# Sample-row fp32 products placed in the four column quarters of the TensorE array

## The chip, the cores and the metric

The kernel runs on one core of a Trainium2 chip. The metric is the device time of one execution in microseconds (us), from the median of several runs. A profile of one execution comes from the hardware profiler; in it PE is the matmul side of TensorE, PEld its weight loads, DVE is VectorE, ACT is ScalarE, POOL is GpSimd, and SP issues most DMAs.

## What is computed

One layer of a hybrid decoder works on 1024 prompt tokens and on 8 sample rows (eight sequences with one new token each), with shared weights. After an RMS norm and a wide input projection come two branches: retention (4 heads, keys of 128, values of 256, with a state matrix per head) and sliding-window attention (16 query heads in 4 groups that share a key/value head, head size 64, window 128). Each branch is normalised or gated and projected; the two are merged and projected again.

The change concerns only the 8 sample rows. Each of them has its own state and its own cache, so that its products share nothing with the other rows:

```python
def retention_chunk(S, q, k, v, lg):            # sample rows: L = 1, S is (8, heads, 128, 256)
    ...
    S_new = exp(L*lg) * S + einsum('bmhd,bmhe,mh->bhde', k, v, k_dec)
    o = ... einsum('bnhd,bhde->bnhe', q, S) ... # per sample: a 1 x 128 row times its 128 x 256 state

def swa_sample(q, k, v, sinks, cache_k, cache_v):
    kk = concatenate([cache_k, k]); vv = concatenate([cache_v, v])
    s = einsum('bnqhgd,bnkhd->bnhgqk', q, kk) * 64**-0.5   # per sample and kv head: 4 x 64 times 64 x 128
    p = softmax(with the sink)                              # 32 rows of 128 per kv head
    return einsum('bnhgqk,bnkhd->bnqhgd', p, vv)            # per sample: 4 x 128 times 128 x 64
```

## The kernel before

Nearly all of the time is the big projections, each product of which is done in three fp32r matmuls (high times high, high times low, low times high). `phase1` makes the normed input, then runs eight groups, four retention heads and four key/value heads of the window branch; `phase23` runs the branch projections and the output projection. Within a group, `groups` appends steps: a gemm for one 128-token tile, the generator steps of the tiles before it (`ret_tile`, `swa_tile`), gate blocks as filler, and the sample rows of the group at one place in it (`ret_rows`, `swa_rows`), which are generators too, advanced one `yield` at a time. The final order of the instructions on each engine is not the order of the code: a scheduler places them by a simulated timeline, and each engine works its own list in order.

The sample rows of a retention head (`ret_rows`, L394 to L447): the row projection, eight outer products into the state (L426, L428), and then in two halves of four samples the products of query and state. All four write to the same 8 rows of PSUM: sample b's weights are an 8-column block, `zq`, that holds its query in column b and zeros elsewhere (made by one multiplication with a mask, L432), and the four are added up in PSUM:

```python
for b in range(H):                                                      # L440
    nc.tensor.matmul(po[:NS, :DV], zq[:, half * H + b, :], st[:, b, :], start=(b == 0), stop=(b == H - 1))
```

The two halves are added on 8 rows (L444, L446), and `head_norm` normalises and transposes them (L339).

The sample rows of a key/value head (`swa_rows`, L573 to L630): queries are transposed (L591) and masked into `zq` (L594), the cached keys of two samples at a time are transposed into a 128 x 128 block (L600). The scores of all 32 rows (8 samples, 4 heads) come from four matmuls that are added up on the same 32 rows of PSUM (L607). After the softmax on 32 rows a transpose (L615), and one matmul of 32 rows against the values of all eight samples, 512 columns (L620), of which a mask (L622) and a sum (L624) keep each row's own 64. The result is transposed (L627) and copied to `oT` (L630).

All operands of L441, L607 and L620 are plain fp32, and each such matmul stands in the trace as two loads and two matmul records: the two passes of one product. Of the big gemms (fp32r) each has one. "128*8" in a row of the profile means 128 rows and 8 columns of the array in use.

Of the kernel before, what the change touches and what calls it, by code (L numbers as in the profile page):

```python
# [12 lines left out]
AF = mybir.ActivationFunctionType  # L13
ALU = mybir.AluOpType
AX = mybir.AxisListType
# [31 lines left out]
MROW = 40  # L47
MLO = 32
KST = 64 + NS

RAW = 3
NA1 = 7
# [20 lines left out]
def shape_constants():  # L73
    c, s = rope_tables(DK)
    out = {}
    cols = SEQ + NS
    ct = np.concatenate([c[:cols].T, c[:cols].T], 0)
    st = np.concatenate([s[:cols].T, -s[:cols].T], 0)
    out["c_ropeT"] = np.stack([ct, st], 1)
    tm = np.concatenate([c, s], 1).reshape(NT + 1, P, 128)  # L80
    tm[NT] *= DK ** -0.5
    out["c_ropeK"] = tm.transpose(1, 0, 2)
    c2, s2 = rope_tables(HD)
    tm = np.concatenate([c2, s2], 1).reshape(NT + 1, P, HD)
# [9 lines left out]
    misc = np.zeros((P, 8 + 8 + 64 + 128 + 8))  # L94
# [5 lines left out]
    misc[:, 16:80] = np.eye(8).reshape(1, 64)  # L100
    z = np.zeros((2, HD, NS // 2, NS, G))
    for b in range(NS):
        z[b % 2, :, b // 2, b, :] = 1.0
    misc[:, 80:208] = z.reshape(P, 128)
    for r in range(NS * G):
        misc[r, 208 + r // G] = 1.0
    out["c_misc"] = misc
    return {k: np.ascontiguousarray(v.astype(np.float32)) for k, v in out.items()}

# [13 lines left out]
class Body:  # L123
# [200 lines left out]
    def head_norm(self, po, p, c, oT, cols):  # L324
        nc = self.nc
        junk = self.t(self.ap, [P, DV], "junk", bufs=1)
        ss = self.t(self.sm, [P, 1], "ss", bufs=4)
        nc.scalar.activation(out=junk[:p], in_=po, func=AF.Square, scale=c, accum_out=ss[:p])
        r = self.rstd(ss[:p], DV, 1, 1.0, p)
        if not isinstance(c, float):  # L330
            f = self.t(self.sm, [P, 1], "fsc", bufs=4)
            nc.vector.tensor_tensor(out=f[:p], in0=r, in1=c, op=ALU.mult)
            r = f[:p]
        on = self.t(self.ap, [P, DV], "on", bufs=1)
        nc.scalar.activation(out=on[:p], in_=po, func=AF.Copy, scale=r)
# [4 lines left out]
        nc.vector.tensor_copy(out=oT[:, :, cols], in_=pt[:, : 2 * P].rearrange("p (i n) -> p i n", i=2)[:, :, :p])  # L340

    def ret_tile(self, h, t, units, qT, st, oT):
        nc = self.nc
# [50 lines left out]
    def ret_rows(self, h, units, qT, oT):  # L394
# [23 lines left out]
        for half in range(2):  # L418
# [9 lines left out]
                nc.vector.scalar_tensor_tensor(out=sl, in0=sl, scalar=self.g1[h], in1=ps[:], op0=ALU.mult, op1=ALU.add)  # L428
            yield
            if half == 0:  # L430
                zq = self.t(self.ap, [P, NS, NS], "zq", bufs=1)
                nc.vector.tensor_tensor(  # L432
                    out=zq[:],
                    in0=qT[:, SEQ:TOK].unsqueeze(1).broadcast_to([P, NS, NS]),
                    in1=self.misc[:, 16:80].rearrange("p (a b) -> p a b", a=NS),
                    op=ALU.mult,
                )
                osum = kv[:, :DV]
            po = self.t(self.pav, [P, 512], "av")
            for b in range(H):  # L440
                nc.tensor.matmul(po[:NS, :DV], zq[:, half * H + b, :], st[:, b, :], start=(b == 0), stop=(b == H - 1))  # L441
            nc.sync.dma_start(out=self.o["rs"][0, bs, h].rearrange("b d e -> d b e"), in_=st[:])
            if half == 0:
                nc.scalar.activation(out=osum, in_=po[:NS, :DV], func=AF.Copy)  # L444
            else:
                nc.vector.tensor_tensor(out=osum, in0=osum, in1=po[:NS, :DV], op=ALU.add)  # L446
        yield from self.head_norm(osum, NS, 1.0, oT, slice(SEQ, TOK))  # L447


    def rope_s(self, dst, src, A, B, nh, t, p=P):  # L450
# [122 lines left out]
    def swa_rows(self, g, units, oT):  # L573
# [18 lines left out]
        zq = self.t(self.ap, [P, NS // 2, NS, G], "zq2", bufs=1)  # L592
        qv = pt[:, : G * NS].rearrange("p (j b) -> p b j", j=G).unsqueeze(1).broadcast_to([P, NS // 2, NS, G])
# [10 lines left out]
        R = NS * G  # L604
# [3 lines left out]
        s = self.t(self.ap, [R, 1, P], "srow", bufs=1)  # L608
        mx = self.t(self.sm, [P, 4], "mx", bufs=2)
        nc.vector.tensor_copy(out=s[:, 0, :], in_=sc[:R, :P])  # L610
        nc.vector.tensor_reduce(out=mx[:R, 0:1], in_=s[:, 0, :], axis=AX.X, op=ALU.max)
        self.softmax_tail(s, [s[:, 0, :]], [1.0], mx[:R, 0:1], self.nsinkr[:, g : g + 1], self.sinkr[:, g : g + 1], R, 1)
# [3 lines left out]
        pTs = self.t(self.ap, [P, R], "pTs", bufs=1)  # L616
        nc.scalar.activation(out=pTs[:], in_=pt[:, :R], func=AF.Copy)
# [5 lines left out]
        os_ = self.t(self.ap, [R, HD], "osr", bufs=1)  # L623
# [4 lines left out]
        pv = pt[:HD, :R].rearrange("p (b i a) -> p i b a", b=NS, i=2)  # L628
        for a in range(2):
            nc.vector.tensor_copy(out=oT[a * HD : (a + 1) * HD, :, SEQ:TOK], in_=pv[:, :, :, a])  # L630

    def swa_tables(self):
        nc = self.nc
# [22 lines left out]
    def build(self):  # L656
# [4 lines left out]
        with tc.tile_pool(name="const", bufs=1, reuse_waits="tile") as cp, tc.tile_pool(name="sm", bufs=2, reuse_waits="tile") as sm, \  # L661
# [9 lines left out]
            self.misc = self.t(cp, [P, 216], "misc")  # L671
# [23 lines left out]
    def groups(self):  # L695
# [157 lines left out]
    def swa_consts(self):  # L853
# [11 lines left out]
        nc.sync.dma_start(out=self.sink[:], in_=self.i["swa_sinks"][0:1, :].broadcast_to([P, SH]))  # L865
        self.nsink = self.t(ap, [P, SH], "nsink")
        nc.vector.tensor_scalar(out=self.nsink[:], in0=self.sink[:], scalar1=-1.0, scalar2=None, op0=ALU.mult)
        self.sinkr = self.t(ap, [NS * G, KVH], "sinkr")
        for b in range(NS):
            nc.sync.dma_start(out=self.sinkr[b * G : (b + 1) * G, :], in_=self.i["swa_sinks"][0].rearrange("(g j) -> j g", g=KVH))  # L870
        self.nsinkr = self.t(ap, [NS * G, KVH], "nsinkr")
# [126 lines left out]
```

## Time and profile before

| | |
|---|---|
| median of 3 runs | 1188.66 us (1185.74 to 1190.13) |
| profiled execution | 1189.96 us, its span 1188.1 us |
| busy: PE / PEld | 1166.6 us / 1103.2 us |
| busy: DVE / ACT / POOL | 644.3 / 438.7 / 429.0 us |
| DMA | mean 98 GB/s, 116.61 MB |
| granted TensorE clock | 0.997 of full speed |

A timeline row reads: start, how long from the first start to the last end, engine, line, operation, output <- inputs, array rows*columns, partitions x elements, count; in brackets, idle time before it and what ended it. A matmul record lasts from its start to its modelled end and overlaps the next one, so what a matmul costs the engine is the distance from its start to the next start.

### The profile page before, as it was taken

What the parts mean: (1) busy time and instruction counts of PE and PEld (TensorE: products, weight loads), DVE (VectorE), ACT (ScalarE), POOL (GpSimd) and SP (SyncE); (2) the same over time, 40 slices, a digit from 0 to 9 for tenths busy, and PEclk for the clock granted to TensorE, in tenths of its full rate; (3) what the DMA queues carried; (4) which work ended last, traced back from release to release, by engine and by line L of the source; (5) the groups of instructions that cost most, each with busy time, mean ns of one, the idle gap of its engine ahead of it and who ended that gap; (6) DMA issues with size and microseconds to landing.
All of it is one profiled execution on the core that took longest, in us unless ns stands there. A gap on an engine that the chain in (4) does not pass through costs nothing.

```text
span 1188.1 us, 19187 instructions
## 1 busy us (share of the span) xinstructions
PE 1166.6 (98%) x7116; PEld 1103.2 (93%) x7116; DVE 644.3 (54%) x1798; ACT 438.7 (37%) x1130; POOL 429.0 (36%) x395
## 2 busy tenths in 40 slices
PE   6999999999999999999999999999999999999998
PEld 5899999999989999999999999999999999999876
DVE  5755545544644386776775677477843411654121
ACT  6533333344234235544463446345544210221010
POOL 5325116215325435533563356235751221221010
PEclk9999999999999999999999999999999999999999
DMA  9224114313123411220141014101537744644221
GB/s 321 59 73 115 60 43 146 113 60 94 49 69 84 136 63 46 74 79 7 59 129 43 10 60 126 47 1 37 174 104 242 232 143 138 187 127 142 74 91 69
DMA packets 125165, 116.61 MB, mean 98 GB/s; under 512 B 17480, under 2 KB 113224, under 8 KB 125040
## 3 DMA queue, kind: packets, MB, share of 16 engines
q1 hardware_dynamic: 118160, 106.93, 29.2%
q10 hardware_dynamic: 6912, 8.46, 2.0%
q8 instruction: 56, 0.92, 0.3%
q14 instruction: 37, 0.30, 0.1%
HBM read 84.98 MB, written 32.44 MB: 99 GB/s over the span
## 4 chain that ended last, share of the span: by engine, by line
PE 92%; DMA 2%; DVE 2%; issue 1%; ACT 1%; POOL 1%; SPq 0%; ACTq 0%; POOLq 0%
PE acc L212 16%; PE acc L213 16%; PE acc L214 16%; PE acc L224 10%; PE acc L223 10%; PE acc L222 10%; PE acc L233 1%; PE acc L232 1%; PE sc L532 1%; PE av L441 1%; PE sc L533 1%; PE av L564 1%; PE av L565 1%; PE tr L544 1%; DMA oT<-d_o 1%
## 5 line engine op out<-in xcount | busy, mean ns | idle before, releaser
L169 POOL TENSOR_TENSOR wlo<-wraw,whi 128x1024 fp32r<-128x1024 f32 (+1 forms) x92 | 206.7, 2253 | 311.7 <-ACT whi L168 268.8
L212 PE MATMUL acc<-hhi,whi 128*128 128x344 f32 x864 | 279.9, 324 | 2.0 <-ACT tg L298 2.0
L214 PE MATMUL acc<-hhi,wlo 128*128 128x344 f32 x864 | 277.5, 322 | 0.0
L213 PE MATMUL acc<-hlo,whi 128*128 128x344 f32 x864 | 277.1, 321 | 0.0
L222 PE MATMUL acc<-whi,hhi 128*128 128x384 f32 x512 | 175.6, 344 | 2.3 <-ACT hhi L139 1.2
L224 PE MATMUL acc<-whi,hlo 128*128 128x384 f32 x512 | 175.3, 342 | 0.0
L223 PE MATMUL acc<-wlo,hhi 128*128 128x384 f32 x512 | 175.3, 343 | 0.0
L212 PEld LDWEIGHTS acc<-hhi,whi 128*128 128x128 f32 x864 | 162.9, 188 | 5.5 <-ACT tg L298 2.6
L213 PEld LDWEIGHTS acc<-hlo,whi 128*128 128x128 f32 x864 | 162.6, 188 | 1.6
L214 PEld LDWEIGHTS acc<-hhi,wlo 128*128 128x128 f32 x864 | 162.6, 188 | 1.6 <-issue 0.4
L168 ACT ACTIVATE whi<-wraw 128x1024 fp32r<-128x1024 f32 (+1 forms) x92 | 90.4, 984 | 177.3 <-PE acc L213 114.3
L147 POOL TENSOR_TENSOR rs<-ms,nhalf 128x1 f32<-128x1 f32 (+3 forms) x81 | 69.4, 858 | 216.7 <-DVE ms L146 192.4
L222 PEld LDWEIGHTS acc<-whi,hhi 128*128 128x128 f32 x512 | 97.5, 191 | 6.1 <-issue 2.5
L224 PEld LDWEIGHTS acc<-whi,hlo 128*128 128x128 f32 x512 | 97.3, 190 | 0.5 <-DVE hlo L140 0.2
L223 PEld LDWEIGHTS acc<-wlo,hhi 128*128 128x128 f32 x512 | 97.4, 190 | 0.4
L288 POOL TENSOR_TENSOR oT<-oT,tg 128x344 f32<-128x344 f32 x48 | 48.3, 1007 | 63.1 <-DVE tg L286 58.6
L486 ACT ACTIVATE s<-sc,ng,rs 128x128 f32<-128x128 f32 x128 | 57.0, 456 | 17.4 <-DVE ng L483 17.3
L224 PE MATMUL acc<-whi,mlo 128*128 128x512 f32 x128 | 50.5, 395 | 0.0
L223 PE MATMUL acc<-wlo,mhi 128*128 128x512 f32 x128 | 50.3, 393 | 0.0
L222 PE MATMUL acc<-whi,mhi 128*128 128x512 f32 x128 | 50.1, 393 | 0.0
L965 DVE TENSOR_TENSOR x<-acc,x 128x512 f32<-128x512 f32 x16 | 11.0, 690 | 68.7 <-PE acc L224 68.7
L286 DVE SCALAR_TENSOR_TENSOR tg<-tg,acc 128x344 f32<-128x344 f32 x48 | 24.5, 511 | 35.7 <-ACT tg L285 35.5
(357 smaller groups left out, 2394.8 us busy)
## 6 DMA issues: line engine op xcount, KB each, us to landing
wraw<-in_w_in SPq DMA_DIRECT2D x36, 512.0 KB
d_t<-tg ACTq DMA_DIRECT2D x48, 172.0 KB
d_o<-oT SPq DMA_DIRECT2D x16, 516.0 KB
tt<-d_t SPq DMA_DIRECT2D x48, 172.0 KB
wraw<-in_w_in SPq DMA_DIRECT2D x32, 256.0 KB
st<-d_o SPq DMA_DIRECT2D x9, 516.0 KB
d_m<-tt SPq DMA_DIRECT2D x24, 172.0 KB
mm<-d_m SPq DMA_DIRECT2D x24, 172.0 KB
```

The costliest lines, as they stand in the source:

```text
L147: nc.gpsimd.tensor_tensor(out=rs[:p, :width], in0=ms[:p, :width], in1=self.nhalf[:p, :width], op=ALU.pow)
L168: nc.scalar.activation(out=hi[:, :f], in_=raw[:, :f], func=AF.Copy)
L169: nc.gpsimd.tensor_tensor(out=lo[:, :f], in0=raw[:, :f], in1=hi[:, :f].bitcast(F32), op=ALU.subtract)
L212: nc.tensor.matmul(ps, whi[:, k, :], hi[:, cs], start=(k == 0), stop=False)
L213: nc.tensor.matmul(ps, whi[:, k, :], lo[:, cs], start=False, stop=False)
L214: nc.tensor.matmul(ps, wlo[:, k, :], hi[:, cs], start=False, stop=(k == KT - 1))
L222: nc.tensor.matmul(ps, hi[:, k, a:b], whi[:, kk, :], start=(k == 0), stop=False)
L223: nc.tensor.matmul(ps, hi[:, k, a:b], wlo[:, kk, :], start=False, stop=False)
L224: nc.tensor.matmul(ps, lo[:, k, a:b], whi[:, kk, :], start=False, stop=(k == KT - 1))
L286: nc.vector.scalar_tensor_tensor(out=tg[:], in0=tg[:], scalar=1.0, in1=ps[:, :BL], op0=ALU.add, op1=ALU.mult)
L288: nc.gpsimd.tensor_tensor(out=sl, in0=sl, in1=tg[:], op=ALU.mult)
L486: nc.scalar.activation(out=s[:p, j, :], in_=src[j], func=AF.Exp, bias=ng[:p, j : j + 1], scale=scale[j], accum_out=l[:p, j : j + 1])
```

## The change

Four products at a time are written to different quarters of the array's columns, 32 columns each (`tile_position=(0, 32 * b)`), and so to different quarters of the 128 PSUM partitions, rather than being added up on the same rows.

- `ret_rows`: `zq` becomes a lasting tile with 32 columns per sample, zeroed once; each head copies its queries into one column of each. Each half's four products go to quarters 0 to 3; half 0 stands in row 0 of a quarter, half 1 in row 1. The copy, the sum and `head_norm` work on 128 partitions, and the transposes of `head_norm` are 128 wide, with two copies that pick the rows.
- `swa_rows`: the scores of one pair of samples go to one quarter (8 of its 32 rows are used); the softmax runs on 128 partitions; the products with the values are four matmuls of 128 columns (the pair's own two values) in four quarters in place of one of 512, and two small operations with per-row selectors take the place of the mask and the sum. Transposes are 128 wide.
- The start of the window branch: `sinkr` has 128 rows and is zeroed before its eight DMAs; `zq2` is zeroed there. The table `c_misc` shrinks from 216 to 20 columns.

The core of the diff:

```diff
+QD = 32
...
+        if cols is not None:
+            nc.vector.tensor_copy(out=oT[:, :, cols], in_=pt[:, : 2 * P].rearrange("p (i n) -> p i n", i=2)[:, :, :p])
+        else:
+            for i in range(2):
+                nc.vector.tensor_copy(
+                    out=oT[:, i, SEQ:TOK].rearrange("p (r b) -> p r b", r=2),
+                    in_=pt[:, i * P : (i + 1) * P].rearrange("p (b r) -> p r b", r=QD)[:, 0:2, :])
...
-                zq = self.t(self.ap, [P, NS, NS], "zq", bufs=1)
-                nc.vector.tensor_tensor(
...
-                osum = kv[:, :DV]
+                for i in range(2):
+                    nc.vector.tensor_copy(out=self.zq[:, i, :, i : i + 1], in_=qT[:, SEQ + i * H : SEQ + (i + 1) * H].unsqueeze(2))
+                osum = self.t(self.ap, [P, DV], "osum", bufs=1)
             po = self.t(self.pav, [P, 512], "av")
             for b in range(H):
-                nc.tensor.matmul(po[:NS, :DV], zq[:, half * H + b, :], st[:, b, :], start=(b == 0), stop=(b == H - 1))
+                qd = slice(b * QD, (b + 1) * QD)
+                nc.tensor.matmul(po[qd, :DV], self.zq[:, half, b, :], st[:, b, :], start=True, stop=True, tile_position=(0, b * QD))
...
-        yield from self.head_norm(osum, NS, 1.0, oT, slice(SEQ, TOK))
+        yield from self.head_norm(osum[:], P, 1.0, oT, None)
...
-        nc.vector.tensor_tensor(out=zq[:], in0=qv, in1=self.misc[:, 80:208].rearrange("p (a b j) -> p a b j", a=NS // 2, b=NS), op=ALU.mult)
+        for e in range(2):
+            nc.vector.tensor_scalar(
+                out=zq[:, :, e * G : (e + 1) * G], in0=pt[:, : G * NS].rearrange("p (j i b) -> p b i j", j=G, b=2)[:, e],
+                scalar1=self.misc[:, 16 + e : 17 + e], scalar2=None, op0=ALU.mult)
...
         for i in range(NS // 2):
-            nc.tensor.matmul(sc[:R, :P], zq[:, i].rearrange("p a b -> p (a b)"), kcT[:, i * P : (i + 1) * P], start=(i == 0), stop=(i == NS // 2 - 1))
+            nc.tensor.matmul(sc[qd(i), :P], zq[:, i, :], kcT[:, i * P : (i + 1) * P], start=True, stop=True, tile_position=(0, i * QD))
...
-        nc.tensor.transpose(out=pt[:, :R], in_=s[:, 0, :], identity=self.ident[:R, :R])
+        nc.tensor.transpose(out=pt[:, :P], in_=s[:, 0, :], identity=self.ident[:])
...
-        nc.tensor.matmul(po[:R], pTs[:], V, start=True, stop=True)
-        od = self.t(self.ap, [R, NS, HD], "rbig", bufs=1)
-        nc.vector.tensor_tensor(out=od[:], in0=po[:R].rearrange("p (b d) -> p b d", b=NS), in1=self.misc[:R, 208:216].unsqueeze(2).broadcast_to([R, NS, HD]), op=ALU.mult)
-        nc.vector.tensor_reduce(out=os_[:], in_=od[:].rearrange("p b d -> p d b"), axis=AX.X, op=ALU.add)
+        for i in range(NS // 2):
+            nc.tensor.matmul(po[qd(i), : 2 * HD], pTs[:, qd(i)], V[:, 2 * i : 2 * i + 2, :], start=True, stop=True, tile_position=(0, i * QD))
+        nc.vector.tensor_scalar(out=os_[:], in0=po[:, 0:HD], scalar1=self.misc[:, 18:19], scalar2=None, op0=ALU.mult)
+        nc.vector.scalar_tensor_tensor(out=os_[:], in0=po[:, HD : 2 * HD], scalar=self.misc[:, 19:20], in1=os_[:], op0=ALU.mult, op1=ALU.add)
...
-        nc.tensor.transpose(out=pt[:HD, :R], in_=os_[:], identity=self.ident[:R, :R])
+        nc.tensor.transpose(out=pt[:HD, :P], in_=os_[:], identity=self.ident[:])
...
+            self.zq = self.t(self.ap, [P, 2, NS // 2, QD], "zq", bufs=1)
+            nc.gpsimd.memset(self.zq[:], 0.0)
...
-        self.sinkr = self.t(ap, [NS * G, KVH], "sinkr")
+        self.sinkr = self.t(ap, [P, KVH], "sinkr")
+        nc.gpsimd.memset(self.sinkr[:], 0.0)
...
+        self.zq2 = self.t(ap, [P, NS // 2, QD], "zq2", bufs=1)
+        nc.gpsimd.memset(self.zq2[:], 0.0)
```

What stands in PE's list at three places is shown below; "x4" is four matmuls in a row, and the line numbers are each kernel's own. The first is a half of a retention head's query products, first before (L441) and then now (L442), among the key and value gemms (`acc`) of a prompt tile:

```order
L224 MATMUL acc_1009<-whi_232,hlo_122 128x384
L222 MATMUL acc_1009<-whi_232,hhi_121 128x384
L441 MATMUL av_860<-st_644,zq_858 8x256 x4
L203 MATMUL sc_906<-Slo_779,qhi_873 128x256
L204 MATMUL sc_906<-Shi_778,qlo_874 128x256
```

```order
L221 MATMUL acc_1012<-whi_234,hhi_121 128x384
L222 MATMUL acc_1012<-wlo_235,hhi_121 128x384
L442 MATMUL av_863<-st_646,zq_147 32x256 x4
L202 MATMUL sc_909<-Slo_781,qhi_876 128x256
L203 MATMUL sc_909<-Shi_780,qlo_877 128x256
```

The four stand one behind the other at the same place; one gemm matmul has moved ahead of them. In both kernels five of the eight halves stand as four in a row and three are split in two and two. The first of the split ones, before and now:

```order
L441 MATMUL av_1696<-st_1494,zq_1694 8x256 x2
L359 MATMUL tr_1705<-ident_63,kr_1563 128x128
L202 MATMUL sc_1648<-vhi_1450,phi_1643 128x256
L203 MATMUL sc_1648<-vlo_1451,phi_1643 128x256
L204 MATMUL sc_1648<-vhi_1450,plo_1644 128x256
L441 MATMUL av_1696<-st_1494,zq_1694 8x256 x2
```

```order
L442 MATMUL av_1701<-st_1498,zq_147 32x256 x2
L364 MATMUL tr_1710<-ident_63,kr_1567 128x128
L201 MATMUL sc_1652<-vhi_1454,phi_1647 128x256
L202 MATMUL sc_1652<-vlo_1455,phi_1647 128x256
L203 MATMUL sc_1652<-vhi_1454,plo_1648 128x256
L338 MATMUL tr_1732<-ident_63,on_1607 128x128
L442 MATMUL av_1701<-st_1498,zq_147 32x256 x2
```

A transpose has slipped in, and the split stays. The third place is the product of the probabilities with the cached values, for the first key/value head, before (L620) and now (L624):

```order
L224 MATMUL acc_6041<-whi_4596,hlo_122 128x384
L620 MATMUL av_5905<-cV_4781,pTs_5725 32x512
L222 MATMUL acc_6041<-whi_4596,hhi_121 128x384
```

```order
L222 MATMUL acc_6056<-wlo_4607,hhi_121 128x384
L545 MATMUL tr_5937<-ident_63,s_5766 128x128 x3
L624 MATMUL av_5918<-cV_4791,pTs_5738 32x128 x4
L545 MATMUL tr_5937<-ident_63,s_5766 128x128
L223 MATMUL acc_6056<-whi_4606,hlo_122 128x384
```

One matmul of 512 columns has become four of 128, here between transposes of a prompt tile. On POOL's list, where the window branch begins, before and now:

```order
L863 MEMSET neg_4809 128x128
L147 TENSOR_TENSOR rs_4887<-ms_4886,nhalf_68 128x5
```

```order
L869 MEMSET neg_4819 128x128
L875 MEMSET sinkr_4825 128x4
L880 MEMSET zq_1173_4835 128x128
L146 TENSOR_TENSOR rs_4900<-ms_4899,nhalf_68 128x5
```

The two new memsets follow the old one; the eight DMAs into `sinkr` on SP now wait for the first of them, and the loads of `cK` and `cV` stand behind those DMAs.

## Rows read from the trace of the kernel before

**Rows 1.** Page: busy time of PE; chain that ended last, by engine.
```profile
PE 1166.6 (98%) x7116; PEld 1103.2 (93%) x7116; DVE 644.3 (54%) x1798; ACT 438.7 (37%) x1130; POOL 429.0 (36%) x395
...
PE 92%; DMA 2%; DVE 2%; issue 1%; ACT 1%; POOL 1%; SPq 0%; ACTq 0%; POOLq 0%
```

**Rows 2.** Busy time by stretch: us, then engines, granted clock, DMA share, GB/s.
```profile
100.00:300.00 200.00, 200.00 (x1268) 190.52 (x1267) 100.30 (x294) 74.78 (x198) 66.86 (x67) 1.00 0.26 82
...
600.00:830.00 230.00, 230.00 (x1441) 219.96 (x1440) 156.75 (x504) 105.43 (x307) 105.46 (x101) 1.00 0.19 58
```

**Rows 3.** Instructions of lines L441, L607, L620: ns min/median/max, first and last start.
```profile
L441 PE MATMUL av<-st,zq x64: 379/379/383, 76.8 to 348.5; 128*8 128x256 f32 x64
...
L607 PE MATMUL sc<-rbig,zq x32: 272/273/297, 461.4 to 798.2; 128*32 128x128 f32 x32
...
L620 PE MATMUL av<-cV,pTs x8: 592/604/617, 492.1 to 825.0; 128*32 128x512 f32 x8
```

**Rows 4.** Timeline of PE at the first half of head 0.
```profile
76.31 0.34 PE L224 MATMUL acc<-whi,hlo 128*128 128x384 f32 x1
76.49 0.34 PE L222 MATMUL acc<-whi,hhi 128*128 128x384 f32 x1
76.76 1.89 PE L441 MATMUL av<-st,zq 128*8 128x256 f32 x8
78.58 0.39 PE L203 MATMUL sc<-Slo,qhi 128*128 128x256 f32 x1
```

**Rows 5.** Timeline of the weight loads in the same stretch.
```profile
76.75 1.39 PEld L441 LDWEIGHTS av<-st,zq 128*8 128x8 f32 x8 [0.26 <-issue]
```

**Rows 6.** Timeline of PE at a half that is split in two and two.
```profile
138.12 1.03 PE L441 MATMUL av<-st,zq 128*8 128x256 f32 x4
139.08 0.33 PE L359 MATMUL tr<-ident,kr 128*128 128x128 f32 x1
```

**Rows 7.** Timeline of PE at the scores of the first key/value head.
```profile
461.44 1.06 PE L607 MATMUL sc<-rbig,zq 128*32 128x128 f32 x8
462.43 0.39 PE L532 MATMUL sc<-kThi,qs 128*128 128x256 f32 x1
```

**Rows 8.** Timeline of PE at the values of the first key/value head.
```profile
492.09 1.04 PE L620 MATMUL av<-cV,pTs 128*32 128x512 f32 x2
493.07 0.44 PE L222 MATMUL acc<-whi,hhi 128*128 128x384 f32 x1
```

**Rows 9.** Timeline of PE at four full transposes and the matmuls behind them.
```profile
451.86 0.60 PE L544 MATMUL tr<-ident,s 128*128 128x128 f32 x4
...
452.45 0.32 PE L213 MATMUL acc<-hlo,whi 128*128 128x344 f32 x1
```

**Rows 10.** Timeline of PE at the transpose of the 32 score rows.
```profile
471.33 0.32 PE L213 MATMUL acc<-hlo,whi 128*128 128x344 f32 x1
471.58 0.25 PE L615 MATMUL tr<-ident,srow 32*128 32x32 f32 x1
...
472.03 0.27 PE L512 MATMUL tr<-ident,kd 128*128 128x128 f32 x1
```

**Rows 11.** Timeline of PE at the transposes of the 8 rows of head 0.
```profile
100.38 0.32 PE L213 MATMUL acc<-hlo,whi 128*128 128x344 f32 x1
100.63 0.28 PE L339 MATMUL tr<-ident,on 8*128 8x8 f32 x2
...
101.17 0.32 PE L212 MATMUL acc<-hhi,whi 128*128 128x344 f32 x1
```

**Rows 12.** Where the window branch begins: POOL, SP, and the first use of cK.
```profile
403.49 0.21 POOL L863 MEMSET neg<- 128x128 f32 x1
...
404.81 0.40 SPq L874 DMA_DIRECT2D cK<-in_cache_swa_k  x1
...
L597 POOL COPY kc<-cK x4: 611/612/613, 433.7 to 774.5; 128x512 f32<-128x512 f32 x4
```

**Rows 13.** PE's longest wait at the start, from its timeline.
```profile
26.13 1.25 PE L271 MATMUL tr<-ident,qT 128*128 128x128 f32 x8 [2.21 <-DVE hlo L140]
```

More of the change, by code (lines that the diff above doesn't have):

```diff
@@ L49 @@
 KST = 64 + NS
+QD = 32
+NMISC = 8 + 8 + 2 + 2
 RAW = 3
@@ L93, in shape_constants @@
     out["c_band"] = (j > i) * 1.0
-    misc = np.zeros((P, 8 + 8 + 64 + 128 + 8))
+    misc = np.zeros((P, NMISC))
     for h in range(RH):
@@ L99, in shape_constants @@
         misc[r : r + 8, 8:16] = np.eye(8)
[L100 to L106, printed above, removed]
+    for r in range(P):
+        misc[r, 16 + r // HD] = 1.0
+        if r % QD < 2 * G:
+            misc[r, 18 + r % QD // G] = 1.0
     out["c_misc"] = misc
@@ L430, in ret_rows @@
             if half == 0:
-                zq = self.t(self.ap, [P, NS, NS], "zq", bufs=1)
-                nc.vector.tensor_tensor(
[L433 to L437, printed above, removed]
-                osum = kv[:, :DV]
+                for i in range(2):
+                    nc.vector.tensor_copy(out=self.zq[:, i, :, i : i + 1], in_=qT[:, SEQ + i * H : SEQ + (i + 1) * H].unsqueeze(2))
+                osum = self.t(self.ap, [P, DV], "osum", bufs=1)
             po = self.t(self.pav, [P, 512], "av")
             for b in range(H):
-                nc.tensor.matmul(po[:NS, :DV], zq[:, half * H + b, :], st[:, b, :], start=(b == 0), stop=(b == H - 1))
+                qd = slice(b * QD, (b + 1) * QD)
+                nc.tensor.matmul(po[qd, :DV], self.zq[:, half, b, :], st[:, b, :], start=True, stop=True, tile_position=(0, b * QD))
             nc.sync.dma_start(out=self.o["rs"][0, bs, h].rearrange("b d e -> d b e"), in_=st[:])
             if half == 0:
-                nc.scalar.activation(out=osum, in_=po[:NS, :DV], func=AF.Copy)
+                nc.scalar.activation(out=osum[:], in_=po[:, :DV], func=AF.Copy)
             else:
-                nc.vector.tensor_tensor(out=osum, in0=osum, in1=po[:NS, :DV], op=ALU.add)
-        yield from self.head_norm(osum, NS, 1.0, oT, slice(SEQ, TOK))
+                nc.vector.tensor_tensor(out=osum[:], in0=osum[:], in1=po[:, :DV], op=ALU.add)
+        yield from self.head_norm(osum[:], P, 1.0, oT, None)
     def rope_s(self, dst, src, A, B, nh, t, p=P):
@@ L603, in swa_rows @@
         yield
[L604 removed]
+        qd = lambda i: slice(i * QD, (i + 1) * QD)
         sc = self.t(self.psc, [P, 512], "sc")
         for i in range(NS // 2):
[L607 to L608 removed]
+            nc.tensor.matmul(sc[qd(i), :P], zq[:, i, :], kcT[:, i * P : (i + 1) * P], start=True, stop=True, tile_position=(0, i * QD))
@@ L609, in swa_rows @@
+        s = self.t(self.ap, [P, 1, P], "srow", bufs=1)
         mx = self.t(self.sm, [P, 4], "mx", bufs=2)
-        nc.vector.tensor_copy(out=s[:, 0, :], in_=sc[:R, :P])
-        nc.vector.tensor_reduce(out=mx[:R, 0:1], in_=s[:, 0, :], axis=AX.X, op=ALU.max)
-        self.softmax_tail(s, [s[:, 0, :]], [1.0], mx[:R, 0:1], self.nsinkr[:, g : g + 1], self.sinkr[:, g : g + 1], R, 1)
+        nc.vector.tensor_copy(out=s[:, 0, :], in_=sc[:, :P])
+        nc.vector.tensor_reduce(out=mx[:, 0:1], in_=s[:, 0, :], axis=AX.X, op=ALU.max)
@@ L613, in swa_rows @@
+        self.softmax_tail(s, [s[:, 0, :]], [1.0], mx[:, 0:1], self.nsinkr[:, g : g + 1], self.sinkr[:, g : g + 1], P, 1)
         yield
         pt = self.t(self.ptr, [P, 512], "tr")
-        nc.tensor.transpose(out=pt[:, :R], in_=s[:, 0, :], identity=self.ident[:R, :R])
-        pTs = self.t(self.ap, [P, R], "pTs", bufs=1)
-        nc.scalar.activation(out=pTs[:], in_=pt[:, :R], func=AF.Copy)
+        nc.tensor.transpose(out=pt[:, :P], in_=s[:, 0, :], identity=self.ident[:])
+        pTs = self.t(self.ap, [P, P], "pTs", bufs=1)
@@ L618, in swa_rows @@
+        nc.scalar.activation(out=pTs[:], in_=pt[:, :P], func=AF.Copy)
         yield
         po = self.t(self.pav, [P, 512], "av")
-        nc.tensor.matmul(po[:R], pTs[:], V, start=True, stop=True)
-        od = self.t(self.ap, [R, NS, HD], "rbig", bufs=1)
-        nc.vector.tensor_tensor(out=od[:], in0=po[:R].rearrange("p (b d) -> p b d", b=NS), in1=self.misc[:R, 208:216].unsqueeze(2).broadcast_to([R, NS, HD]), op=ALU.mult)
-        os_ = self.t(self.ap, [R, HD], "osr", bufs=1)
-        nc.vector.tensor_reduce(out=os_[:], in_=od[:].rearrange("p b d -> p d b"), axis=AX.X, op=ALU.add)
+        for i in range(NS // 2):
+            nc.tensor.matmul(po[qd(i), : 2 * HD], pTs[:, qd(i)], V[:, 2 * i : 2 * i + 2, :], start=True, stop=True, tile_position=(0, i * QD))
@@ L629, in swa_rows @@
+        pv = pt[:HD, :P].rearrange("p (u r) -> p u r", r=QD)[:, :, : 2 * G].rearrange("p u (b i a) -> p i u b a", b=2, i=2)
         for a in range(2):
-            nc.vector.tensor_copy(out=oT[a * HD : (a + 1) * HD, :, SEQ:TOK], in_=pv[:, :, :, a])
+            for i in range(2):
+                nc.vector.tensor_copy(out=oT[a * HD : (a + 1) * HD, i, SEQ:TOK].rearrange("p (u b) -> p u b", b=2), in_=pv[:, i, :, :, a])
     def swa_tables(self):
@@ L670, in build @@
             self.d_m = [self.t(dp, [P, TOK], f"d_m{k}") for k in range(8)]
-            self.misc = self.t(cp, [P, 216], "misc")
+            self.misc = self.t(cp, [P, NMISC], "misc")
             rng = self.t(cp, [P, KT], "rng")
@@ L867, in swa_consts @@
         nc.vector.tensor_scalar(out=self.nsink[:], in0=self.sink[:], scalar1=-1.0, scalar2=None, op0=ALU.mult)
-        self.sinkr = self.t(ap, [NS * G, KVH], "sinkr")
+        self.sinkr = self.t(ap, [P, KVH], "sinkr")
+        nc.gpsimd.memset(self.sinkr[:], 0.0)
         for b in range(NS):
-            nc.sync.dma_start(out=self.sinkr[b * G : (b + 1) * G, :], in_=self.i["swa_sinks"][0].rearrange("(g j) -> j g", g=KVH))
-        self.nsinkr = self.t(ap, [NS * G, KVH], "nsinkr")
+            r = b // 2 * QD + b % 2 * G
+            nc.sync.dma_start(out=self.sinkr[r : r + G, :], in_=self.i["swa_sinks"][0].rearrange("(g j) -> j g", g=KVH))
+        self.zq2 = self.t(ap, [P, NS // 2, QD], "zq2", bufs=1)
+        nc.gpsimd.memset(self.zq2[:], 0.0)
+        self.nsinkr = self.t(ap, [P, KVH], "nsinkr")
         nc.vector.tensor_scalar(out=self.nsinkr[:], in0=self.sinkr[:], scalar1=-1.0, scalar2=None, op0=ALU.mult)
```

6 lines of the change are left out of this document (2 added, 4 removed).

## The prediction

> **What bounds the kernel.** I read the page's busy times and its chain of waits first, then the stretches, then the timeline of PE around the three lines that the change moves. PE is busy for 1166.6 of 1188.1 us, and 92% of the chain that ended last is PE's own work [rows 1]. In the stretches that hold the sample rows of both branches, PE is busy for the whole 200 of 200 us and 230 of 230 us, at the full granted clock, while DVE, ACT and POOL are idle for a third to two thirds of the time [rows 2]. So a microsecond less of matmuls there is a microsecond less of the whole, and work taken off or put on DVE, ACT and POOL is worth nothing as long as PE doesn't wait for it.
>
> **What the three lines cost PE now.** L441 has 64 passes (32 products of two), L607 has 32 (16 products), L620 has 8 (four products) [rows 3].
> - A half of four samples: L441 starts at 76.76 and the next matmul at 78.58, 1.82 us [rows 4]. Its eight passes follow each other at (1.89 - 0.38) / 7 = 0.216 us, since the merged row spans the first start to the last end and one pass lasts 0.379 [rows 3, 4]. Eight times 0.216 is 1.73; the other 0.09 is an empty moment at the exit. There is one of the same size at the entry: the 384-column matmul ahead takes from 76.49 to 76.76, 0.27, where the one before it took 0.18 [rows 4]. So the group pays some 0.18 us for coming and going, already now.
> - A group of two samples: 138.12 to 139.08, 0.96 us [rows 6].
> - By PE's list five halves stand as four and three as two and two: 5 x 1.82 + 6 x 0.96 = 14.9 us.
> - L607: 461.44 to 462.43, 0.99 us for eight passes of 128 columns, (1.06 - 0.27) / 7 = 0.11 us apart [rows 3, 7]; four heads, 4.0 us.
> - L620: 492.09 to 493.07, 0.98 us for two passes of 512 columns [rows 8]; 3.9 us over four heads.
>
> Together 22.8 us of 1188.
>
> **What four column quarters can do.** The change removes no pass: L441 and L607 have as many as before, L620's two of 512 columns become eight of 128. It can only let passes run side by side. The trace of before shows no two quarters in use, so the price is bounded from both sides: no overlap at all (0 saved here) and all four quarters at once (below). The value I take follows from the order in the list. The two passes of one product stand one behind the other and use the same quarter, and passes of one quarter run one after the other, as all eight of L441 do now, 0.216 apart. PE takes its list in order. So the second pass of sample 0 waits for the first; once it runs, the first pass of sample 1, in another quarter, can start beside it; and so on. Eight passes fit in 5 slots rather than 8, four passes in 3 rather than 4.
> - L441: five groups save 3 x 0.216, six save 1 x 0.216: 3.24 + 1.30 = 4.5 us.
> - L607: 4 x 3 x 0.11 = 1.3 us.
> - L620: what is now 0.98 becomes L607's 0.99 less 3 x 0.11, that is 0.66: 4 x 0.32 = 1.3 us.
>
> Sum 7.1 us. I take this middle value rather than an end, since both ends ask for something that the list or the rows speak against.
>
> The Trainium skill, "TensorE: Matmul & The Clock Gate", Part 3 (packing small matmuls), says that matmuls keep strict order while column tiles overlap, and gives 2.38 times for three column quarters. By that factor alone the some 19.4 us of passes in the three lines (22.8 less 19 groups at 0.18) would fall by an estimated 11.2 us; no run here shows it, and it isn't said there for products of two passes that share a quarter.
>
> **What the wider transposes do.** A full 128-wide transpose is cheap: four of them and one 344-column matmul take from 451.86 to 452.45, 0.59 us, or 0.11 each with 0.16 for the matmul [rows 9]. The narrow ones of the sample rows are dear: from 471.33 to 472.03, 0.70 us, go one 344-column matmul, L615 and two full transposes, which by those prices are 0.16 + 2 x 0.11 = 0.38; so L615 costs 0.32 [rows 10]. At 128 rows it should cost 0.11: 0.21 saved, four times, 0.8 us. L627 is of the same kind (32 rows); I price it the same, 0.8 us. L339's pair of 8 rows: 100.38 to 101.17, 0.79 us, hold two 344-column matmuls, the pair and one full transpose; 0.79 - 0.32 - 0.11 = 0.36, and as two full ones 0.22: 0.14 saved, 0.6 us over four heads [rows 11]. Sum 2.2 us. If a 128 by 64 transpose stays as dear as now, L627's 0.8 is lost; that is the lower bound of this term, 1.4.
>
> **What is hidden.** DVE loses the mask multiplications and the sum over 512 columns and gains small copies, ACT's copies are as long in columns as before, POOL gains three memsets. All of it lies beside a PE that is full [rows 2]; 0 us. The first memset runs before the first x tile is there. The other two stand behind the memset of `neg`, which ends at 403.70 [rows 12]; the eight DMAs into `sinkr` wait for one, so that `cK`, issued at 404.81 now, goes out some 2.5 us later, with all that SP has behind it. Its first user on POOL starts at 433.7 [rows 12], so 26 us cover it; without that cover it would cost the 2.5 us, once. At the start the order of two input tiles' transposes shifts around PE's longest wait, 2.21 us at 26.13 [rows 13]. It can shrink or grow by its own size: 0 taken, 2 us to either side for the range.
>
> **The sum.** 7.1 + 2.2 = 9.3 us off the profiled execution: 1189.96 - 9.3 = 1180.7. That execution is 1.3 us above the median of the runs, so on the median's scale 1179.4. Bounds of this case: 2 us to either side for the start, 0.8 for L627: 1177 to 1182.5.
>
> **The rivals.**
> 1. Quarters don't overlap: passes of different quarters run one behind the other as those of one quarter do. For it: nothing in the trace shows two passes at once. Then L441 and L607 stay, L620's eight passes cost 0.99 for 0.98, and only the transposes save: 1188.7 - 2.2 = 1186.5. If each change of quarter also costs the 0.09 of an exit [rows 4], there are 5 x 3 + 6 x 1 + 4 x 3 + 4 x 3 = 45 changes, 4.1 us, and it is 1190.6. Both are within 0.5%, which is 5.9 us and about what a measurement of this kernel can tell from no change. That the change doesn't do what it says is this case.
> 2. All four at once: the engine keeps the quarters apart and a product needs two slots in all. Against it: the second pass of sample 0 stands ahead of sample 1's first. Then a group of any size takes two slots: L441 saves 5 x 6 x 0.216 + 6 x 2 x 0.216 = 9.1, L607 4 x 6 x 0.11 = 2.6, L620 4 x 0.65 = 2.6; with the transposes 16.5 us, 1172.2.
> 3. Slower: a quarter's weights can't be loaded while a matmul of another quarter runs, so that at each of the 45 changes the array runs empty (0.09) and the load of 32 columns stands open. That load is bounded by how much of L607's slot it can fill, 0.11. 45 x 0.20 = 9.0 us, less 2.2: 1195.5. It is slower by over 0.5% from 0.18 us a change on. Against it: the eight loads of L441 now run from 76.75 to 78.14, each beside a pass of its own group, the last of them done before the last pass starts at 76.76 + 7 x 0.216 = 78.27 [rows 4, 5].
>
> The same page and part says that a weight load overlaps matmuls in flight only where the row groups differ; all four quarters share them, so by that rule the third rival would be the one. Rows 5 speak against the rule within one quarter; no row shows it between two.
>
> **How the numbers follow.** The forecast has 0.50; no overlap 0.27; all at once 0.10; slower 0.10; 0.03 for something between no overlap and the forecast (about 1183, half of it faster). Faster by over 0.5% is below 1182.7: 0.50 x 0.93 + 0.10 + 0.015 = 0.58. Slower by over 0.5%: 0.10. The rest, 0.32, is within. The predicted time is the forecast's, 1179.4. The range leaves out the slower rival and the tails and takes in the others: 1171.5 to 1190.5; the forecast's own is 1177 to 1182.5.
>
> **What would show it.** In the timeline of after, the four-sample group should take about 1.17 us to the next start (1.82 now), the starts of the second pass of one sample and the first of the next nearly coinciding and pairs 0.216 apart; the scores about 0.66 us. Eight starts 0.216 apart are the first rival, all within two slots the second, gaps of 0.3 us or more between them with loads that start only after a pass has ended the third. The transpose of the score rows should cost 0.11. PE's busy time should fall by about as much as the span. The prediction is wrong if PE waits at 26 or at 403 to 434 us where it didn't, or if the three lines save less than 4 us.

## The result, and the profile after

The changed kernel takes 1173.88 us (median of four runs, 1171.80 to 1174.98); the kernel before took 1188.70 in four runs on the same chip (1185.74 to 1190.13). The ratio is 0.9876 [0.9853, 0.9900], 14.8 us less (11.9 to 17.5). The forecast was 1179.4 us, 9.3 us less by the profiled execution: the sign held and the time lies in the stated range, but only because that range was drawn to take in the second rival. The forecast's own range, 1177 to 1182.5, does not hold it, and the mechanism is that of the second rival, which had a chance of 0.10.

The profiled execution took 1171.8 us. Its page, busy times and the chain that ended last, to be held against [rows 1]:

```profile
PE 1148.1 (98%) x7140; PEld 1095.1 (94%) x7140; DVE 638.6 (55%) x1818; ACT 436.8 (37%) x1130; POOL 428.3 (37%) x398
...
PE 90%; DVE 3%; DMA 2%; issue 2%; POOL 1%; ACT 1%; SPq 0%; ACTq 0%; POOLq 0%; DVEq 0%
```

The span fell from 1188.1 to 1170.0 us, PE's busy time from 1166.6 to 1148.1, and PE still bounds the kernel. The three lines of [rows 3] have new numbers, L442, L610 and L624 (ns min/median/max, first and last start):

```profile
L442 PE MATMUL av<-st,zq x64: 378/392/404, 74.2 to 336.5; 128*32 128x256 f32 x64
...
L610 PE MATMUL sc<-rbig,zq x32: 272/284/298, 450.1 to 780.7; 128*32 128x128 f32 x32
...
L624 PE MATMUL av<-cV,pTs x32: 272/285/298, 479.4 to 807.5; 128*32 128x128 f32 x32
```

One pass is not shorter than before (medians 0.392, 0.284 and 0.285 us, where L441 had 0.379 and L607 0.273). What changed is how the passes lie in time. PE's timeline after, at the first half of head 0 (for [rows 4]), at a half split in two and two [rows 6], at the scores [rows 7] and at the values [rows 8] (start, duration from first start to last end):

```profile
73.91 0.34 PE L222 MATMUL acc<-wlo,hhi 128*128 128x384 f32 x1
74.18 0.64 PE L442 MATMUL av<-st,zq 128*32 128x256 f32 x8
74.75 0.39 PE L202 MATMUL sc<-Slo,qhi 128*128 128x256 f32 x1
...
132.66 0.63 PE L442 MATMUL av<-st,zq 128*32 128x256 f32 x4
133.22 0.33 PE L364 MATMUL tr<-ident,kr 128*128 128x128 f32 x1
...
450.07 0.43 PE L610 MATMUL sc<-rbig,zq 128*32 128x128 f32 x8
450.43 0.44 PE L222 MATMUL acc<-wlo,hhi 128*128 128x384 f32 x1
...
479.39 0.42 PE L624 MATMUL av<-cV,pTs 128*32 128x128 f32 x8
479.75 0.33 PE L545 MATMUL tr<-ident,s 128*128 128x128 f32 x1
```

The eight passes lie between 74.18 and 74.75: 0.57 us to the next start, where it was 1.82, and two quarters (132.66 to 133.22) take as long as four. With one pass at 0.39, the last one starts 0.64 - 0.39 = 0.25 after the first: two rounds. The same timeline, cut off at 74.22, shows what has begun within 0.04 us:

```profile
74.18 0.42 PE L442 MATMUL av<-st,zq 128*32 128x256 f32 x4
```

and the weight loads of the whole group, for [rows 5]:

```profile
74.18 0.16 PEld L442 LDWEIGHTS av<-st,zq 128*32 128x32 f32 x8 [0.25 <-issue]
```

Four passes start almost together (in the records 7, 7 and 6 ns apart); the other four start the same way, 0.24 us after the first. The eight loads are through within 0.16 us, beside each other and beside the passes, where one lasts 0.106 to 0.109. The scores and the values take 0.36 us each, where they took 0.99 and 0.98. The empty moments of about 0.09 us at entry (73.91 to 74.18 is 0.27, where a 384-column matmul takes 0.18) and exit are as before; the one at entry lies ahead of the first start and so outside the 0.57, the one at exit inside it. Over all groups, first start to next start: 6.2 + 1.4 + 1.4 = 9.0 us, where the three lines took 22.8. That is 13.7 us (unrounded), the forecast's term being 7.1.

The transposes, from the same view: L618 for [rows 10], L630 (the old L627), L338 for [rows 11]:

```profile
460.50 0.27 PE L618 MATMUL tr<-ident,srow 128*128 128x128 f32 x1
460.61 0.38 PE L512 MATMUL tr<-ident,qr 128*128 128x128 f32 x2
...
483.76 0.28 PE L630 MATMUL tr<-ident,osr 128*64 128x128 f32 x1
483.79 0.40 PE L212 MATMUL acc<-hlo,whi 128*128 128x344 f32 x1
484.03 0.32 PE L213 MATMUL acc<-hhi,wlo 128*128 128x344 f32 x1
...
96.42 0.38 PE L338 MATMUL tr<-ident,on 128*128 128x128 f32 x2
96.64 0.27 PE L364 MATMUL tr<-ident,kr 128*128 128x128 f32 x1
```

0.11 for L618, 0.22 for a pair of L338; L630 and a 344-column matmul take 483.76 to 484.03, 0.27, less 0.16 is 0.11. All are as priced: 2.2 us, and the 64-column one is not dear. PE's waits in the changed kernel (sum, times, longest):

```profile
PE tr L270 <- DVE hlo L139: 3.5, 5, 1.5
...
PE sc L533 <- ACT kThi L138: 0.9, 1, 0.9
PE tr L545 <- DVE s L491: 0.8, 1, 0.8
...
PE acc L221 <- DVE vv L139: 0.2, 1, 0.2
```

They sum to 17.9 us, and to 17.8 before. Within that sum waits have changed place: `kThi` and `s` are waited for in the window branch, 1.7 us, where it was 0.2, and one of 0.9 for `opA6l` has gone; the longest one for `hlo` is 1.5 where it was 2.21 [rows 13].

The two profiles differ by 18.2 us, the medians by 14.8. In the profiled execution of before TensorE had the lower clock twice. Of before, then of after, the same stretches (length in us; busy time and count of PE, PEld, DVE, ACT and POOL; granted clock, DMA share, GB/s):

```profile
27.70:31.10 3.40, 3.40 (x13) 3.40 (x12) 2.52 (x12) 2.99 (x7) 0.08 (x1) 0.50 1.13 307
48.20:51.60 3.40, 3.40 (x13) 2.48 (x12) 1.31 (x7) 0.75 (x3) 0.00 (x0) 0.50 0.02 5
```

```profile
27.70:31.10 3.40, 3.40 (x24) 3.18 (x23) 3.40 (x16) 3.16 (x9) 2.07 (x3) 1.00 1.13 306
48.20:51.60 3.40, 3.40 (x23) 3.22 (x22) 0.59 (x3) 0.38 (x1) 0.00 (x0) 1.00 0.02 5
```

A clock of 0.50 is 1.2 GHz. By estimate half of 2 x 3.4 us, 3.4, is lost there (13 matmuls in a stretch where after has 23 or 24). The first of the stretches follows PE's wait of 2.21 us, which is two shorter ones after, 0.58 and 1.03. The second can't be put down to the change: the wait of 1.5 us ahead of it stands in after too, and five runs below with the changed kernel's start (twice, three times and four times the products, in groups and in turn, and no split halves) have a stretch of 3.4 us at half clock at 46.5 to 48.1. 18.2 - 3.4 = 14.8, against 13.7 + 2.2 = 15.9 from the groups and the transposes; the 1.1 us between are not placed.

### The profile page after: what moved, and what is told of

It is laid out like the page before. It is cut to its first block, busy times and chain, and to the rows that moved or that the text cites. A ratio compares the mean times of both kernels' runs of the same rounds, so it can differ in the third digit from the quotient of the medians.

```text
span 1170.0 us, 19270 instructions
## 1 busy us (share of the span) xinstructions
PE 1148.1 (98%) x7140; PEld 1095.1 (94%) x7140; DVE 638.6 (55%) x1818; ACT 436.8 (37%) x1130; POOL 428.3 (37%) x398
## 4 chain that ended last, share of the span: by engine, by line
PE 90%; DVE 3%; DMA 2%; issue 2%; POOL 1%; ACT 1%; SPq 0%; ACTq 0%; POOLq 0%; DVEq 0%
PE acc L211 16%; PE acc L212 15%; PE acc L213 15%; PE acc L221 10%; PE acc L223 10%; PE acc L222 10%; PE acc L231 1%; PE acc L232 1%; PE sc L533 1%; PE sc L534 1%; PE av L565 1%; PE av L566 1%; PE tr L545 1%; DMA oT<-d_o 1%; POOL wlo L168 1%
```

## The experiments

Those with an interval were timed in five rounds beside the kernel before, whose median was 1190.18 us beside the first four and 1188.69 beside the version beyond the change; the others are one profiled execution each.

**Each branch alone.** The kernel before with the change to the retention branch only (`zq`, L441, `head_norm`):

```diff
-                nc.tensor.matmul(po[:NS, :DV], zq[:, half * H + b, :], st[:, b, :], start=(b == 0), stop=(b == H - 1))
+                nc.tensor.matmul(po[qd, :DV], self.zq[:, half, b, :], st[:, b, :], start=True, stop=True, tile_position=(0, b * QD))
```

> The part of the change in the retention rows alone (quarters for the query products, head_norm on 128 partitions); the window branch is as before. Theory side by side (passes in different quarters run at once, so that a group lasts as long as the passes of its fullest quarter): the query products fall from 14.9 to 6.2 us as in the profile of after, and the two transposes per head save 0.6: 9.3 us, 1179.4. Rival (most of the gain comes from elsewhere, such as the start's order and clock or the lighter VectorE work of the window branch): 1184 or more.

Measured 1180.07 us, 0.9914 [0.9896, 0.9933], 10.2 us less. And with the change to `swa_rows` only:

```diff
-            nc.tensor.matmul(sc[:R, :P], zq[:, i].rearrange("p a b -> p (a b)"), kcT[:, i * P : (i + 1) * P], start=(i == 0), stop=(i == NS // 2 - 1))
+            nc.tensor.matmul(sc[qd(i), :P], zq[:, i, :], kcT[:, i * P : (i + 1) * P], start=True, stop=True, tile_position=(0, i * QD))
...
-        nc.tensor.matmul(po[:R], pTs[:], V, start=True, stop=True)
+            nc.tensor.matmul(po[qd(i), : 2 * HD], pTs[:, qd(i)], V[:, 2 * i : 2 * i + 2, :], start=True, stop=True, tile_position=(0, i * QD))
```

> The part in the window branch alone (quarters for scores and values, softmax on 128 partitions, wide transposes); the retention rows are as before. Side by side: scores and values fall from 7.9 to 2.9 us, the transposes save 1.6: 6.6 us, of which the waits that are new in the profile of after near 492 and 819 us give back some 1.5 us: 1183 to 1184. Rival (gain from elsewhere): under 1181, or no gain at all if those waits eat it, 1188.

Measured 1184.22, 0.9949 [0.9935, 0.9964], 6.1 us less. The parts sum to 16.3, the whole gave 14.8 with an interval of 11.9 to 17.5: each works by itself, and within the noise they add up. By the traces, 8.7 us of groups and 0.6 of transposes come off in the first, 5.0 and 1.6 in the second. The new waits for `kThi` (1.0) and `s` (0.8) stand in the second's profile; in the first's, `kThi` has 0.2 as before.

**The rest of the change without the quarters.** The weights are padded with zeros to the full 128 columns and the products added up:

```diff
-                nc.tensor.matmul(po[qd, :DV], self.zq[:, half, b, :], st[:, b, :], start=True, stop=True, tile_position=(0, b * QD))
+                nc.tensor.matmul(po[c0 : c0 + 128, :DV], self.zq[:, half, b, :], st[:, b, :], start=(b * QD % 128 == 0), stop=((b + 1) * QD % 128 == 0), tile_position=(0, c0))
```

> As after, but the weights of the query products and of the scores are 128 columns wide, zero outside a sample's quarter, and the four products are added up over the whole array; the result stands in the same places. Values stay in quarters. Side by side: no two passes at once, so the query products take 64 passes at 0.216 = 13.8 us for 6.2 and the scores 32 at 0.109 = 3.5 for 1.4: after plus 9.7 us, 1183.6. There should be no empty moment at a group's entry and exit. Rival (gain from the wider transposes and other engines): as after, 1174.

Measured 1186.38, 0.9967 [0.9955, 0.9980], 3.9 us less than before, and 2.8 us above what was expected (1.3 when the higher median of the before-runs, 1190.18 for 1188.70, is allowed for). PE's timeline at the first half:

```profile
75.38 0.34 PE L222 MATMUL acc<-wlo,hhi 128*128 128x384 f32 x1
75.55 1.89 PE L444 MATMUL av<-st,zq 128*128 128x256 f32 x8
77.09 0.47 PE L202 MATMUL sc<-Slo,qhi 128*128 128x256 f32 x1
```

Full-width passes follow each other 0.216 apart like the 8-column ones of before, so width alone gives nothing. But the moment at entry is gone (75.38 to 75.55, 0.17), and the next matmul comes in before the eighth slot is over. The whole time says less than the group, since this run has a wait that neither kernel has, 4.0 us up to 899.8, with a stretch at half clock behind it (900.1 to 903.5):

```profile
PE acc L211 <- ACT tg L297: 5.3, 3, 4.0
```

**Halves in place of quarters.** Samples 0 and 1 add up in one half of 64 columns, 2 and 3 in the other:

```diff
-                nc.tensor.matmul(po[qd, :DV], self.zq[:, half, b, :], st[:, b, :], start=True, stop=True, tile_position=(0, b * QD))
+                nc.tensor.matmul(po[c0 : c0 + 64, :DV], self.zq[:, half, b, :], st[:, b, :], start=(b * QD % 64 == 0), stop=((b + 1) * QD % 64 == 0), tile_position=(0, c0))
```

> As after, but the query products and the scores are put in two halves of the array (64 columns each), two products added up in each half. Side by side: a group of four takes 4 slots of 0.216 rather than 2, and a group of two, whose products share a half, 4 as well: 11 x 0.86 = 9.5 us, plus 0 to 2.0 for entries and exits, for 6.2; the scores 4 x 0.44 = 1.8, plus 0 to 0.7, for 1.4. After plus 3.7 to 6.3: 1177.6 to 1180.2. If the passes keep the order of the list so strictly that a waiting one holds up the next, a group of four needs 7 slots or more: 1182 or more.

Measured 1188.20, 0.9985 [0.9973, 0.9997], a miss in the whole and a hit in the group. The timeline, cut at 74.23 and then whole:

```profile
74.21 0.44 PE L444 MATMUL av<-st,zq 128*64 128x256 f32 x2
...
74.21 1.09 PE L444 MATMUL av<-st,zq 128*64 128x256 f32 x8
75.23 0.38 PE L202 MATMUL sc<-Slo,qhi 128*128 128x256 f32 x1
```

Two passes have begun within 0.02 us. Passes of one half start over 0.2 us apart, so that the second can only be sample 2's, though sample 0's second pass and both of sample 1's stand ahead of it and use the other half. The group takes four rounds, 1.02 us. The line savings are 3.7 + 1.6 + 2.5 us and the transposes' 2.2; what ate them stands in the waits, 4.7 us up to 900.9, which the changed kernel doesn't have, and two longer ones for `kThi` and `s`:

```profile
PE acc L211 <- ACT tg L297: 5.7, 3, 4.7
...
PE sc L535 <- ACT kThi L138: 1.9, 2, 1.5
PE tr L547 <- DVE s L493: 1.5, 2, 1.3
```

and in a granted clock of 0.50 that began within the longest, from 898.6 to 905.4. In both runs PE stood there for `tg` on ACT, whose instruction stood behind one (`opA6h`) that waited for the DMA `oT<-d_o`, 4.78 us with full width and 5.45 with halves. That wait of ACT alone is not what sets these two apart: it is 4.78 in the kernel before and 3.81 in the changed one, and neither holds PE for `tg` there. Why PE is held in these two was not tried.

**How far does PE look past a waiting pass?** Each query product is done twice, three times or four times, those of one sample one behind the other (0 0 1 1 2 2 3 3, and so on):

```diff
-                nc.tensor.matmul(po[qd, :DV], self.zq[:, half, b, :], st[:, b, :], start=True, stop=True, tile_position=(0, b * QD))
+                for again in range(2):
+                    nc.tensor.matmul(po[qd, :DV], self.zq[:, half, b, :], st[:, b, :], start=True, stop=True, tile_position=(0, b * QD))
```

> As after, but each query product of the retention rows stands twice, one behind the other (quarters 0 0 1 1 2 2 3 3), so that four passes of one quarter stand ahead of the next quarter's first. Theory look-ahead (a pass that waits for its quarter doesn't hold up passes of other quarters behind it): the 16 passes of a group go in four rounds of four starts some 7 ns apart, 0.57 + 2 x 0.216 = 1.00 us to the next start. Rival strict order (a pass that waits holds up all behind it, and after got its two rounds only since its passes stand in that order): 13 slots, 12 x 0.216 + 0.31 = 2.9 us.

1176.84 us. The timeline, cut at 75.80, then whole:

```profile
75.71 0.44 PE L443 MATMUL av<-st,zq 128*32 128x256 f32 x4
...
75.71 1.09 PE L443 MATMUL av<-st,zq 128*32 128x256 f32 x16
76.73 0.38 PE L202 MATMUL sc<-Slo,qhi 128*128 128x256 f32 x1
```

Four passes begin in the first round; one is of sample 3, with twelve passes of three quarters ahead of it in the list. 16 passes in four rounds, 1.02 us; in strict order it would be 2.9.

> Each query product stands four times, one behind the other (0 0 0 0 1 1 1 1 ...), so that 8, 16 and 24 passes with as many loads stand ahead of the first pass of quarters 1, 2 and 3. Look-ahead without a limit in reach: 8 rounds of four, 0.57 + 6 x 0.216 = 1.87 us. Look-ahead of limited depth: the later quarters start late, and the group takes between 1.87 us and the 29 slots of strict order, 6.4 us; how many quarters start in the first round tells the depth.

1204.73 us, and 4.52 for the group, neither 1.87 nor 6.4: a look-ahead of limited depth. The timeline, cut at 76.66, cut at 76.70, and whole:

```profile
75.81 1.05 PE L443 MATMUL av<-st,zq 128*32 128x256 f32 x4
...
75.81 1.30 PE L443 MATMUL av<-st,zq 128*32 128x256 f32 x6
...
75.81 4.59 PE L443 MATMUL av<-st,zq 128*32 128x256 f32 x32
80.33 0.39 PE L202 MATMUL sc<-Slo,qhi 128*128 128x256 f32 x1
```

Four passes run alone, and only with quarter 0's fifth does quarter 1 begin (four become six in 0.04 us); 4.52 us in all. In that fifth round quarter 0 has one pass running and three waiting, as every quarter had in the run before. So the rule would be that PE looks past three waiting passes of a quarter and no more: each next quarter starts four rounds later, 8 + 3 x 4 = 20 rounds. Two runs tested it:

> The changed kernel with every query product of the samples done three times, the three of one sample one behind the other (000 111 222 333; 24 passes for a group of four). Theory from the two runs before it: PE starts passes of a later quarter past at most three waiting passes of one quarter. With twice the products (four passes to a quarter) all quarters then start in the first round and the group takes four rounds; with four times (eight passes) each next quarter starts four rounds after the one ahead, 8 + 3 x 4 = 20 rounds of 0.216, plus 0.18 for entry and exit = 4.50 us, and 4.52 was measured. With three times (six passes) each next quarter starts two rounds later: 6 + 3 x 2 = 12 rounds, 2.59 + 0.18 = 2.77 us from the first start to the next matmul; the split groups of two, 6 + 2 = 8 rounds, 1.91. Rival, a limit on the whole number of passes looked past (twelve or so) and not on those of one quarter: quarters 0 and 1 start in the first round, 2 two rounds later or so, some 8 to 9 rounds, 1.9 to 2.1 us. No limit that matters: 6 rounds, 1.48 us. Strict order: 24 - 3 = 21 rounds, 4.7 us.

1190.19 us. Cut at 76.20, and whole:

```profile
75.71 0.86 PE L443 MATMUL av<-st,zq 128*32 128x256 f32 x4
...
75.71 2.87 PE L443 MATMUL av<-st,zq 128*32 128x256 f32 x24
78.51 0.39 PE L202 MATMUL sc<-Slo,qhi 128*128 128x256 f32 x1
```

2.80 us against 2.77 expected (the 0.18 in that sum is put down to entry and exit, but the time runs from the first start, so that it holds only the exit's 0.09; the rest, in the records, is the few hundredths by which a later quarter's starts lag behind). 0.49 us after the first start four passes have begun, two of quarter 0 alone, then its third together with quarter 1's first, as the rule has it. The groups of two took 1.87 (1.91 expected). The last run does the four products in turn over the samples:

```diff
-            for b in range(H):
+            for b in [b for again in range(4) for b in range(H)]:
```

> The changed kernel with every query product of the samples done four times as in the run that took 4.52 us, but in turn over the samples (0123 0123 0123 0123) and not in groups. The same 32 passes. If three waiting passes of one quarter is the limit, it is never met here: eight rounds of four, 8 x 0.216 + 0.16 to 0.18 = 1.89 to 1.91 us for a whole group of 16 products. If the time is set by the number of passes or of their loads, and not by their order, it stays at 4.5 us.

1184.90 us.

```profile
75.84 1.93 PE L442 MATMUL av<-st,zq 128*32 128x256 f32 x32
77.70 0.39 PE L202 MATMUL sc<-Slo,qhi 128*128 128x256 f32 x1
```

1.86 us for the same 32 passes that took 4.52 in groups: the order makes the difference. Over the whole program that is 1204.73 - 1184.90 = 19.8 us, and the groups differ by 37.15 - 16.55 = 20.6.

**A version beyond the change.** The halves are no longer split in two and two (half 1's queries are put into `zq` only after its state's update), and one full transpose takes the place of four 8-row ones in `swa_rows`:

```diff
+            with self.tc.issue_after(new.ins):
+                nc.vector.tensor_copy(out=self.zq[:, half, :, half : half + 1], in_=qT[:, SEQ + half * H : SEQ + (half + 1) * H].unsqueeze(2))
...
-        for j in range(G):
-            nc.tensor.transpose(out=pt[:, j * NS : (j + 1) * NS], in_=qn[:, j].rearrange("p a b -> p (a b)"), identity=self.ident[:NS, :NS])
+        nc.tensor.transpose(out=pt[:, :P], in_=qn[:].rearrange("p a b -> p (a b)"), identity=self.ident[:])
```

> After with two further edits that lie on PE: each half's copy of the queries comes behind the half's second state update, so that no half is split in two and two (11 groups become 8); and the queries of a key/value head are put at rows 0, 32, 64 and 96 of one zeroed tile, so that one full transpose takes the place of four of 8 rows. Side by side: 3 x (0.55 + 0.09 for the entry) = 1.9 us less for the groups, and 4 x (0.34 + 0.2 - 0.14) = 1.6 for the transposes: 3.5 us under after. The same if other waits take it over: 0 to 1.

Beside it ran the changed kernel once more:

> The changed kernel itself, beside the others on the same chip: 0.985 to 0.990 of before.

1172.92 us (0.9863 [0.9840, 0.9886]) and 1172.51 (0.9869 [0.9848, 0.9891]): the changed kernel came out as expected, and the version beyond it is no faster, where 3.5 us were expected. The query products did fall, from 6.2 to 4.6 us (eight groups of 0.57). PE's waits after 480 us in this version:

```profile
PE acc L221 <- DVE vv L139: 1.3, 1, 1.3
PE sc L533 <- ACT kThi L138: 1.1, 1, 1.1
PE acc L211 <- ACT opA6h L892: 1.0, 1, 1.0
PE acc L212 <- DVE opA6l L893: 0.9, 1, 0.9
```

`vv` held PE for 0.2 in the changed kernel, and the two `opA6` ones were not among its waits. PE's waits are 20.8 us in all, 18.7 in the profile of the run beside it: 2.1 us given back. Its profile also has two stretches of 3.4 us at half clock (from 48.1 and from 891.1, the second right behind the two `opA6` waits), which the profile of the run beside it doesn't have; an estimated half of them, 3.4 us, is lost in that execution. None of the versions beats the changed kernel.

## Why the prediction was right and wrong, step by step

- **PE bounds the kernel, and what is taken off it comes off the whole:** right. 13.7 + 2.2 us of groups, 14.8 us of median.
- **"PE takes its list in order. So the second pass of sample 0 waits for the first [...] Eight passes fit in 5 slots rather than 8":** this is the step that failed. That passes of one quarter run one after the other was right: the passes of 256 columns are 0.21 to 0.24 us apart in the quarters of every run, and at most 0.27 in the halves. That those behind them must wait too was taken from nothing but the order of the list. The halves and the doubled products show passes that start ahead of waiting ones: 16 passes, 0 0 1 1 2 2 3 3, took 1.02 us, where the strict order of this step would need 2.9. Eight passes take two slots, and so do four, not 5 and 3. This put the 7.1 us at half of the 13.7 measured. The second rival had the mechanism and the sum (14.3 + 2.2 = 16.5); the argument against it, that the second pass of sample 0 stands ahead, is the one refuted.
- **The empty moments of 0.09 us at entry and exit stay:** right: 0.09 ahead of a group's 0.57 us and 0.09 within it. The run at full width is without the one at entry.
- **First rival, no overlap; third rival, loads that can't run beside another quarter's matmul:** both refuted by the first four starts and the eight loads within 0.16 us. The rule of the Trainium skill, "TensorE: Matmul & The Clock Gate", Part 3, that a load overlaps matmuls in flight only where row groups differ, does not hold here, since the four quarters share their rows. The same part's strict order of matmuls does not hold between column quarters of such products either: four starts within 0.04 us with passes of other quarters ahead in the list.
- **Transposes, 2.2 us:** right, the 64-column one included.
- **DVE, ACT, POOL and SP are hidden:** nearly. The later `cK` cost nothing, PE's waits between 380 and 480 us are the same two as before (0.6 and 1.2). The window branch got 1.5 us of new waits for `kThi` and `s`, which the forecast put at 0, and lost others of like size.
- **Start, 2 us to either side:** it gained. The wait of 2.21 us became two of 0.58 and 1.03, so that the longest is now 1.5, and the half-clock stretch behind it is not in after's profile. The three profiles with the wait of 2.2 us (before and each branch alone) have that stretch, from 26.1 to 27.7 on; the nine others have none there.

## What to carry to other kernels

Small fp32 products in four column quarters cost as many rounds as the fullest quarter has passes, and a group pays its 0.18 us for coming and going once: so fill all four quarters and keep the group together (here that took 1.6 us off the groups and nothing off the whole, so look at the waits as well). Order the products in turn over the quarters when a quarter gets more than two of them; up to four passes of a quarter in a row did no harm, six cost twice the rounds and eight two and a half times. Before a serial order is written into a sum, look for a row that shows the engine keeping it; the order of the list is not such a row.

## What the runs showed of the hardware that was not expected

- TensorE starts a pass past waiting ones of another column quarter, as long as at most three of one quarter wait: 0.57 us (2 passes a quarter), 1.02 (4), 2.80 (6), 4.52 (8); in turn, 1.86 for 8. That it is three is worked out from these five groups; a queue was not seen itself.
- Coming to a group of quarters or halves costs 0.09 us, and leaving it the same; going to full-width products of the same kind costs nothing at entry (0.17 to the first start, as for a 384-column matmul).
- PE's waits of 2.21 and 4.0 us were followed by a stretch of 3.4 us at 1.2 GHz, and within the wait of 4.7 us one of 6.8 began. Shorter waits are no sure sign: behind the one of 1.5 us at 45 to 47 us, which all twelve profiles have, eight have such a stretch and four have none.
